# Opening loop of a hybrid conv/retention block: VectorE in place of GpSimd, ScalarE for scale and shift, part of the modulation as one-column matmuls

## The chip, the cores and the metric

The kernel runs on one core of one Trainium2 chip. The metric is device time in microseconds (us): the time of one execution as the runs report it. For the kernel before, three runs were timed. The profile comes from one further execution on the chip. Its engines are TensorE (PE, with weight loads listed apart as PEld), VectorE (DVE), ScalarE (ACT), GpSimd (POOL) and SyncE (SP), which issues the DMA transfers here.

## The reference

One layer of an encoder, batch 1, 2048 tokens, width 1024, float32 throughout. What matters here is its first part:

```python
mod = silu(c) @ w_ada + b_ada                 # 1024 -> 6 * 1024
shift1, scale1, gate1, shift2, scale2, gate2 = split(mod, 6)
h = rms_norm(x, g_pre_mix) * (1.0 + scale1) + shift1
xin, b_gate, c_gate, q, k, v, g = split(h @ w_in)     # seven groups of 512 columns
```

Behind it come a short causal convolution, a chunked retention with rotary q and k, an output projection, and an MLP with a squared ReLU, each with its modulation, norm and residual. The modulation is a vector of 1024 numbers per part: the whole row of `silu(c)` times a column of `w_ada`, so a sum over 1024 products for each.

## The kernel before, in words

Tokens are worked in four blocks of 512. The width of 1024 is split into eight k tiles of 128 partitions. A GEMM of a 128x128 weight tile with a 128x512 moving tile is done as three matmuls in a rounded float32 form, on the high and low halves of both operands: line 142 is high by high, line 143 high by low, line 144 low by high. In the opening the activations h are the stationary operand, so that line 143 uses the low half of the weights (`wlo`) and line 144 the low half of h. The trace names the other operand as well: `g<-wlo,r` is line 143.

The opening is the block of code under the pool `st`, for the first 512 tokens. It runs as follows.

- The eight tiles of x, transposed, are loaded (line 277). ScalarE squares each (line 280), VectorE adds the squares up in `sacc` (line 282), and four one-column matmuls with a column of ones (line 285) give the sum of squares of each token.
- `rstd` makes the inverse root: VectorE scales (line 125), GpSimd takes the power of -0.5 (line 127). `spread` lays it out along the tokens: VectorE multiplies the identity by it, four 128x128 pieces (line 223), one matmul with ones (line 227) spreads it over all partitions, ScalarE copies it to `rb` (line 229).
- `mod1(kt)` makes the scale and shift sums of k tile kt. It loads two tiles of 128 x 4 x 256 numbers of `w_ada` (tag `ada`, eight buffers, line 193) and VectorE multiplies each of the eight 128x256 pieces by one column of `silu(c)` and adds them up in `pt` (lines 197 and 199). The sum over the partitions is left to TensorE.
- `mod1_end(kt, pt)` sums `pt` over the partitions by two one-column matmuls (line 207; the profile shows them as four records, since each float32 matmul has two), one for the scale and one for the shift, into two columns of `modps`. All eight k tiles share this one PSUM bank, and the matmuls of a tile wait until the columns before have been read. VectorE then makes `a1 = (sum + 1 + b) * g_pre_mix` (line 210) and `sh1 = sum + b` (line 214).
- `h0_tile(k, pts)` calls `mod1_end`, multiplies the tile of x by `rb` (line 296: VectorE for tile 0, GpSimd for the other seven), and lets ScalarE make h = x * a1 + sh1 twice, as the rounded high half and in full (line 299). VectorE subtracts them to the low half (line 303).
- `startup_weights(kp)` loads the V and K weights of two k tiles (two tiles of 128x1024, line 134). ScalarE rounds them to the high half (line 136), and GpSimd subtracts to the low half (line 138). K weights come from `st` with two buffers, V weights from `wp` with three.
- The loop over the eight k tiles then does seven GEMM groups for each, into seven PSUM banks that stay open over all eight: V for four token tiles and K for three, 7 x 3 matmuls a tile. The call of `h0_tile(k + 1)` stands behind the second group, that of `mod1(k + 2)` ahead of the first.

Each engine works through its own instructions in an order that is fixed before the run. The framework's scheduler chooses it, by an estimate of when each instruction can start and by the order of the program among those that can; a line further down the program may go first. In the trace, for instance, VectorE does four products of tile 0 (from 13.38 us) ahead of line 125. SyncE also issues in order: a load that waits for its buffer holds those behind it.

Behind the opening come the copies of V (line 555), the rotary tables on VectorE (from line 362, in memory that the opening's pools give back), the rotary itself (lines 530 and 539) and the remaining GEMMs of the first block. Some loads are tied to the last load of `mod1` (`last`) by `issue_after`.

Of the kernel before, what the change touches and what calls it, by code (L numbers as in the profile page):

```python
# [11 lines left out]
F32 = mybir.dt.float32  # L12
F32R = mybir.dt.float32r
I32 = mybir.dt.int32
AF = mybir.ActivationFunctionType
ALU = mybir.AluOpType

P = 128
# [3 lines left out]
NK = D // P  # L22
# [12 lines left out]
XIN, BG, CG, QQ, KK, VV, GG = range(7)  # L35
# [19 lines left out]
def block_kernel(  # L55
# [5 lines left out]
    nc = tc.nc  # L61
    PS = bass.MemoryType.PSUM

    keep = ctx.enter_context(tc.tile_pool(name="keep", bufs=1))
# [12 lines left out]
    def nm(s):  # L77
        n_of[s] = n_of.get(s, 0) + 1
        return f"{s}_{n_of[s]}"

    def tmp(shape=(P, 512), dt=F32):
        name = nm("tmp")
        return tp.tile(list(shape), dt, tag="tmp" + "ab"[n_of["tmp"] % 2], name=name, bufs=4)
# [10 lines left out]
    def bank(shape=(P, 512)):  # L94
        return gp.tile(list(shape), F32, tag="g", name=nm("g"))

    def mbank(shape=(P, 512)):
        return mp.tile(list(shape), F32, tag="m", name=nm("m"))
# [4 lines left out]
    ones = keep.tile([P, P], F32, name="ones")  # L103
# [11 lines left out]
    bcol_sb = keep.tile([P, 4, NK], F32, name="bcol_sb")  # L115
    nc.sync.dma_start(bcol_sb, bcol)
    gcol_sb = keep.tile([P, 2, NK], F32, name="gcol_sb")
    nc.sync.dma_start(gcol_sb, gcol)
    sc = keep.tile([P, NK], F32, name="sc")
    nc.scalar.activation(sc, c_sb, AF.Silu)  # L120

    def rstd(ss, n, inv, tag):

        ms = small([P, n], tag + "m")
        nc.vector.tensor_scalar(ms, ss, inv, EPS, op0=ALU.mult, op1=ALU.add)
        r = small([P, n], tag + "r")
        nc.gpsimd.tensor_tensor(r, ms, negh[:, 0:n], op=ALU.pow)
        return r


    def wgroup(src, eng=None, pool=None):
        pool, n = (wp, 3) if pool is None else (pool, 2)
        raw = pool.tile([P, 1024], F32, tag="raw", name=nm("raw"), bufs=n)
        nc.sync.dma_start(raw, src)
        hi = pool.tile([P, 1024], F32R, tag="whi", name=nm("whi"), bufs=n)
        nc.scalar.copy(hi, raw)  # L136
        lo = pool.tile([P, 1024], F32R, tag="wlo", name=nm("wlo"), bufs=n)
        (eng or nc.vector).tensor_tensor(lo, raw, hi.bitcast(F32), op=ALU.subtract)  # L138
        return hi, lo

    def mm3(ps, ah, al, bh, bl, first, last):
        nc.tensor.matmul(ps, ah, bh, start=first, stop=False)  # L142
        nc.tensor.matmul(ps, ah, bl, start=False, stop=False)  # L143
        nc.tensor.matmul(ps, al, bh, start=False, stop=last)  # L144
# [34 lines left out]
    bs1 = keep.tile([P, NK], F32, name="bs1")  # L179
# [3 lines left out]
    a1 = keep.tile([P, NK], F32, name="a1")  # L183
    sh1 = keep.tile([P, NK], F32, name="sh1")
    a2 = keep.tile([P, NK], F32, name="a2")
    sh2 = keep.tile([P, NK], F32, name="sh2")

    def mod1(kt):

        pt = st.tile([P, 256], F32, tag="pt", name=nm("pt"), bufs=4)  # L190
        for i in range(2):
            raw = st.tile([P, 4, 256], F32, tag="ada", name=nm("ada"), bufs=8)
            last = nc.sync.dma_start(raw, ada1[kt, i].rearrange("p (k c) -> p k c", k=4))
            for k in range(4):
                c_ = sc[:, 4 * i + k : 4 * i + k + 1]
                if i == k == 0:
                    nc.vector.tensor_scalar(pt, raw[:, k, :], c_, None, op0=ALU.mult)
                else:
                    nc.vector.scalar_tensor_tensor(  # L199
                        pt, raw[:, k, :], c_, pt, op0=ALU.mult, op1=ALU.add  # L200
                    )
        return pt, last

    def mod1_end(kt, pt):
        ps = modps[:, 2 * kt : 2 * kt + 2]
        for w in range(2):
            nc.tensor.matmul(
                ps[:, w : w + 1], pt[:, w * P : w * P + P], ones[:, 0:1], start=True, stop=True
            )
        nc.vector.scalar_tensor_tensor(  # L210
            a1[:, kt : kt + 1], ps[:, 0:1], bs1[:, kt : kt + 1], gcol_sb[:, 0, kt : kt + 1],
            op0=ALU.add, op1=ALU.mult,
        )
        nc.vector.tensor_tensor(
            sh1[:, kt : kt + 1], ps[:, 1:2], bcol_sb[:, 0, kt : kt + 1], op=ALU.add
        )


    def spread(r):

        dg = tmp()
        for t in range(NT):
            nc.vector.tensor_scalar(
                dg[:, t * P : t * P + P], ident, r[:, t : t + 1], None, op0=ALU.mult
            )
        ps = mbank()
        nc.tensor.matmul(ps, ones, dg, start=True, stop=True)
        rb = tmp()
        nc.scalar.copy(rb, ps)
        return rb  # L230
# [20 lines left out]
    def h_(tag, dt=F32R):  # L251
        return hp.tile([P, 512], dt, tag=tag, name=nm(tag), bufs=HP[tag])
# [19 lines left out]
    with tc.tile_pool(name="st", bufs=NK) as st:  # L272
        xts = []
        sacc = st.tile([P, TB], F32, tag="sacc", name="sacc", bufs=1)
        for k in range(NK):
            xt = st.tile([P, TB], F32, tag="x0", name=nm("x0"))
            nc.sync.dma_start(xt, xT[k * P : k * P + P, 0:TB])
            xts.append(xt)
            sq = sacc if k == 0 else tmp()
            nc.scalar.activation(sq, xt, AF.Square)  # L280
            if k > 0:
                nc.vector.tensor_tensor(sacc, sacc, sq, op=ALU.add)
        ps = mbank()
        for t in range(NT):
            nc.tensor.matmul(
                ps[:, t : t + 1], sacc[:, t * P : t * P + P], ones[:, 0:1], start=True, stop=True
            )
        rb = spread(rstd(ps[:, 0:NT], NT, 1.0 / D, "r1"))
        modps = mbank()
        extra = mbank()  # L290

        def h0_tile(k, pts):
            mod1_end(k, pts)
            h = tmp()
            eng = nc.vector if k == 0 else nc.gpsimd
            eng.tensor_tensor(xts[k], xts[k], rb, op=ALU.mult)
            hi = h_("r" if k < 5 else "wh")
            for o in (hi, h):
                nc.scalar.activation(
                    o, xts[k], AF.Identity, scale=a1[:, k : k + 1], bias=sh1[:, k : k + 1]  # L300
                )
            lo = h_("r" if k < 5 else "wl")
            nc.vector.tensor_tensor(lo, h, hi.bitcast(F32), op=ALU.subtract)
            h_cur.append((hi, lo))


        def startup_weights(kp):
            return [wgroup(win[c * 4 + kp], nc.gpsimd, pool) for c, pool in ((VV, None), (KK, st))]

        pts, _ = mod1(0)  # L310
        ws = startup_weights(0)
        nxt, last = mod1(1)
        h0_tile(0, pts)
        start_ps = [bank() for _ in range(6)] + [extra]
        for k in range(NK):
            if k % 2 == 0 and k > 0:
                ws = startup_weights(k // 2)
            pts = nxt
            if k + 2 < NK:
                nxt, last = mod1(k + 2)  # L320
            c = slice(k % 2 * 512, k % 2 * 512 + 512)
            xh, xl = h_cur[k]
            for i, (w, t) in enumerate([(0, t) for t in range(NT)] + [(1, t) for t in range(3)]):
                if i == 2 and k + 1 < NK:
                    h0_tile(k + 1, pts)
                s = slice(t * P, t * P + P)
                hi, lo = ws[w]
                mm3(start_ps[i], xh[:, s], xl[:, s], hi[:, c], lo[:, c], k == 0, k == NK - 1)
# [5 lines left out]
    def at(tag, shape=(P, 512), dt=F32, bufs=4):  # L334
        pool = {"yh": pl, "yl": pl, "kT": late, "sg": late}.get(tag, pa)
        return pool.tile(list(shape), dt, tag=tag, name=nm(tag), bufs=bufs)
# [178 lines left out]
    with pa_stack:  # L515
# [30 lines left out]
        for b in range(NB):  # L546
# [72 lines left out]
            for t in range(NT):  # L619
                ps = mbank()  # L620
                for h in range(H):
                    s = slice(h * P, h * P + P)
# [4 lines left out]
                if b * NT + t < SEQ // P - 1:  # L627
                    ps = mbank()
                    for h in range(H):
                        s = slice(h * P, h * P + P)  # L630
# [4 lines left out]
                    else:  # L635
                        for h in range(H):
                            s = slice(h * P, h * P + P)
# [4 lines left out]
                for h in range(H):  # L642
                    s = slice(h * P, h * P + P)
# [21 lines left out]
            for j, ps in enumerate(gemm_t(w_in(CG), h_cur)):  # L665
# [4 lines left out]
                c_ = at("qT")  # L670
# [9 lines left out]
            for t in range(NT):  # L680
# [5 lines left out]
                for h in range(H):  # L686
                    s = slice(h * P, h * P + P)
                    o = slice(t * P, t * P + P)
# [23 lines left out]
            for ch, tag in enumerate(("kT", "sg")):  # L712
# [7 lines left out]
                if ch == 0:  # L720
# [3 lines left out]
                    if b + 1 < NB:  # L724
                        rb = spread(r1)
# [448 lines left out]
```

## Time and profile before

| | before |
|---|---|
| median of three runs | 2238.92 us (2238.62 to 2243.34) |
| profiled execution, its own time | 2240.46 us |
| profiled execution, span first to last instruction | 2238.7 us |
| TensorE matmul busy | 2143.6 us (96%) |
| VectorE busy | 1442.8 us (64%) |
| ScalarE busy | 989.9 us (44%) |
| GpSimd busy | 586.7 us (26%) |
| TensorE's mean granted clock | 0.988 |

In the rows of the profile, L138 is line 138 of the kernel; `out<-in` are the program's names without buffer numbers; x8 is a count of instructions; in the timeline the first two numbers are start and length in us, and a bracket tells how long the engine had been idle and what ended that. A start of a matmul is exact, its end is modelled, so that matmuls in a stream seem to overlap: their pace is read from start to start. In the waits, a row is "engine tile line <- engine tile line" with the total, the number of waits and the longest. Times inside the kernel are counted from the first instruction.

### The profile page before, as it was taken

The page shows a single profiled execution, that of the slowest core. Times are in us where ns is not written, and L with a number is a line of the kernel's source. Part 1 is how long each engine was busy: PE and PEld are TensorE (multiplying, and loading weights), DVE is VectorE, ACT ScalarE, POOL GpSimd, SP SyncE. Part 2 cuts the span into 40 slices and gives each one's busy share as a digit, 9 for nine tenths or more (in the row PEclk, how much of TensorE's full clock was granted, in tenths as well). Part 3 has the DMA queues.
Part 4 walks back from the last instruction along what each step waited for, and adds up shares of the span by engine and source line. Part 5 has one row for each costly group of instructions (what it writes and reads, how often), then busy time and mean ns, then how long its engine had stood idle before and what let it go on. Part 6 is the DMA issues. An engine that isn't in the chain of part 4 may idle for free.

```text
span 2238.7 us, 28424 instructions
## 1 busy us (share of the span) xinstructions
PE 2143.6 (96%) x9736; PEld 1765.9 (79%) x9736; DVE 1442.8 (64%) x2198; ACT 989.9 (44%) x1714; POOL 586.7 (26%) x441
## 2 busy tenths in 40 slices
PE   3999999999999999989999999999999999999997
PEld 2787877878787888867888878888888888888885
DVE  7766845675567634776666687556776666555566
ACT  3332532244224522466555556444445555454453
POOL 4132254314423351243333300001433333010012
PEclk8999999999999999999999999999999999999999
DMA  7356467546655563566444477666764443666666
GB/s 283 132 179 220 157 229 242 177 143 214 212 174 202 182 229 129 200 209 217 150 151 148 135 231 219 204 194 192 259 229 155 150 154 120 211 190 197 196 191 242
DMA packets 197426, 428.23 MB, mean 191 GB/s; under 512 B 22560, under 2 KB 22560, under 8 KB 197280
## 3 DMA queue, kind: packets, MB, share of 16 engines
q1 hardware_dynamic: 197280, 426.41, 57.7%
q8 instruction: 76, 1.25, 0.2%
q14 instruction: 70, 0.57, 0.1%
HBM read 322.51 MB, written 103.81 MB: 190 GB/s over the span
## 4 chain that ended last, share of the span: by engine, by line
PE 67%; DMA 11%; issue 10%; DVE 7%; POOL 3%; ACT 1%; SPq 0%; DVEq 0%; POOLq 0%; ACTq 0%
PE g L142 20%; PE g L143 20%; PE g L144 20%; DMA w2r<-in_w 2%; DMA w2d<-w2r 2%; DMA fw<-fd 2%; PE m L142 2%; PE m L143 2%; PE m L144 2%; POOL w2r L502 2%; DMA ada<-in_ada 1%; DMA x<-in_x 1%; DVE pt L199 1%; DVE wl L807 1%; DVE ql L807 1%
## 5 line engine op out<-in xcount | busy, mean ns | idle before, releaser
L143 PE MATMUL g<-ql,wh 128*128 128x512 f32 x896 | 350.9, 392 | 9.6 <-DVE ql L807 9.6
L144 PE MATMUL g<-qh,wl 128*128 128x512 f32 x896 | 350.9, 392 | 0.5 <-DVE wl L807 0.4
L142 PE MATMUL g<-qh,wh 128*128 128x512 f32 x896 | 350.2, 391 | 0.1
L136 ACT CAST whi<-raw 128x1024 fp32r<-128x1024 f32 x148 | 155.3, 1052 | 348.5 <-PE g L144 178.4
L872 DVE TENSOR_TENSOR q<-g,q 128x512 f32<-128x512 f32 x267 | 178.4, 687 | 174.8 <-PE g L144 174.6
L138 DVE TENSOR_TENSOR wlo<-raw,whi 128x1024 fp32r<-128x1024 f32 x140 | 187.6, 1344 | 152.2 <-ACT whi L136 151.7
L807 DVE TENSOR_TENSOR fl<-fw,fh 128x512 fp32r<-128x512 f32 x218 | 161.3, 741 | 162.5 <-ACT fh L806 160.3
L143 PE MATMUL g<-wl,fh 128*128 128x512 f32 x680 | 265.3, 390 | 0.3 <-DVE wl L807 0.3
L144 PE MATMUL g<-wh,fl 128*128 128x512 f32 x680 | 264.6, 389 | 0.0
L806 ACT CAST fh<-fw 128x512 fp32r<-128x512 f32 x218 | 135.2, 620 | 225.8 <-DMA fw<-fd 213.1
L806 ACT CAST wh<-r 128x512 fp32r<-128x512 f32 x224 | 138.8, 620 | 214.7 <-PE g L143 188.7
L142 PE MATMUL g<-wh,fh 128*128 128x512 f32 x680 | 218.4, 390 | 0.8 <-ACT wh L806 0.8
L143 PEld LDWEIGHTS g<-ql,wh 128*128 128x128 f32 x896 | 169.0, 189 | 46.6 <-DVE ql L807 11.5
L144 PEld LDWEIGHTS g<-qh,wl 128*128 128x128 f32 x896 | 169.1, 189 | 36.3 <-DVE wl L807 1.9
L142 PEld LDWEIGHTS g<-qh,wh 128*128 128x128 f32 x896 | 169.3, 189 | 36.1 <-ACT qh L806 0.7
L807 DVE TENSOR_TENSOR wl<-fw,wh 128x512 fp32r<-128x512 f32 x218 | 156.2, 717 | 44.7 <-ACT wh L806 42.2
L1005 POOL TENSOR_TENSOR q<-q,gg 128x512 f32<-128x512 f32 x28 | 43.4, 1577 | 533.4 <-ACT q L1002 285.3
L807 DVE TENSOR_TENSOR wl<-r,wh 128x512 fp32r<-128x512 f32 x224 | 163.6, 731 | 11.0 <-ACT wh L806 10.8
L806 ACT CAST wh<-fw 128x512 fp32r<-128x512 f32 x218 | 135.0, 619 | 65.3 <-PE g L144 30.3
L890 POOL TENSOR_TENSOR r<-r,r 128x512 f32<-128x512 f32 x32 | 41.4, 1294 | 431.8 <-DVE wl L807 384.3
L143 PEld LDWEIGHTS g<-wl,fh 128*128 128x128 f32 x680 | 127.6, 188 | 29.4 <-DVE wl L807 2.9
L142 PEld LDWEIGHTS g<-wh,fh 128*128 128x128 f32 x680 | 127.4, 188 | 28.2 <-ACT wh L806 2.0
(257 smaller groups left out, 4448.6 us busy)
## 6 DMA issues: line engine op xcount, KB each, us to landing
raw<-in_win SPq DMA_DIRECT2D x116, 512.0 KB, 4.2
fd<-q SPq DMA_DIRECT2D x224, 256.0 KB, 2.2
fw<-fd SPq DMA_DIRECT2D x224, 256.0 KB, 2.8
r<-in_w SPq DMA_DIRECT2D x128, 256.0 KB, 4.7
fw<-w2d SPq DMA_DIRECT2D x128, 256.0 KB, 3.0
ada<-in_ada SPq DMA_DIRECT2D x48, 512.0 KB, 4.7
fw<-in_w SPq DMA_DIRECT2D x96, 256.0 KB, 3.6
w2r<-in_w SPq DMA_DIRECT2D x32, 512.0 KB, 5.4
```

Of the source, the lines that this page charges most:

```text
L136: nc.scalar.copy(hi, raw)
L138: (eng or nc.vector).tensor_tensor(lo, raw, hi.bitcast(F32), op=ALU.subtract)
L142: nc.tensor.matmul(ps, ah, bh, start=first, stop=False)
L143: nc.tensor.matmul(ps, ah, bl, start=False, stop=False)
L144: nc.tensor.matmul(ps, al, bh, start=False, stop=last)
L199: nc.vector.scalar_tensor_tensor(pt, raw[:, k, :], c_, pt, op0=ALU.mult, op1=ALU.add)
L502: nc.gpsimd.tensor_tensor(o, a, b_, op=ALU.subtract)
L806: nc.scalar.copy(hi, src)
L807: nc.vector.tensor_tensor(lo, src, hi.bitcast(F32), op=SUB)
L872: (eng or nc.vector).tensor_tensor(o, a, b_, op=ADD)
L890: nc.gpsimd.tensor_tensor(b11, b12, b11, op=SUB)
L1005: eng.tensor_tensor(c, c, gg[1][:, j * 512 : j * 512 + 512], op=ALU.mult)
```

## The change

- `mod1(kt)` now sums only the first n of the eight products on VectorE, n = 4, 4, 6, 7, 7, 8, 8, 8 for k tiles 0 to 7. The rest stay as raw pieces of the loaded tiles.
- `mod1_end` takes those raw pieces to TensorE: for each, and for scale and shift, a one-column matmul of the 128x128 piece with its column of `silu(c)`, accumulated with the sum of `pt` in the same PSUM column. That is twelve products, 24 matmuls.
- `a1` and `sh1` are made on ScalarE, from PSUM: `a1` as sum * g + (1 + b) * g, for which VectorE makes `bs1g = bs1 * g` once at the start, and `sh1` as sum + b.
- The scaling of x by `rb` is done on VectorE for all eight tiles. It is called in `scaled(k)`, ahead of `mod1(k)`, no more in `h0_tile`.
- The weight differences of `startup_weights` are made on VectorE.

```diff
--- before.py
+++ after.py
@@ -185,35 +185,42 @@
     a2 = keep.tile([P, NK], F32, name="a2")
     sh2 = keep.tile([P, NK], F32, name="sh2")
 
+    bs1g = keep.tile([P, NK], F32, name="bs1g")
+    nc.vector.tensor_tensor(bs1g, bs1, gcol_sb[:, 0, :], op=ALU.mult)
+
     def mod1(kt):
 
+
+        n = NK - (4, 4, 2, 1, 1, 0, 0, 0)[kt]
         pt = st.tile([P, 256], F32, tag="pt", name=nm("pt"), bufs=4)
+        raws = []
         for i in range(2):
             raw = st.tile([P, 4, 256], F32, tag="ada", name=nm("ada"), bufs=8)
             last = nc.sync.dma_start(raw, ada1[kt, i].rearrange("p (k c) -> p k c", k=4))
-            for k in range(4):
-                c_ = sc[:, 4 * i + k : 4 * i + k + 1]
-                if i == k == 0:
-                    nc.vector.tensor_scalar(pt, raw[:, k, :], c_, None, op0=ALU.mult)
-                else:
-                    nc.vector.scalar_tensor_tensor(
-                        pt, raw[:, k, :], c_, pt, op0=ALU.mult, op1=ALU.add
-                    )
-        return pt, last
-
-    def mod1_end(kt, pt):
+            raws += [raw[:, k, :] for k in range(4)]
+        for k, raw in enumerate(raws[:n]):
+            c_ = sc[:, k : k + 1]
+            if k == 0:
+                nc.vector.tensor_scalar(pt, raw, c_, None, op0=ALU.mult)
+            else:
+                nc.vector.scalar_tensor_tensor(pt, raw, c_, pt, op0=ALU.mult, op1=ALU.add)
+        return (pt, list(enumerate(raws))[n:]), last
+
+    def mod1_end(kt, parts):
+        pt, raws = parts
         ps = modps[:, 2 * kt : 2 * kt + 2]
         for w in range(2):
-            nc.tensor.matmul(
-                ps[:, w : w + 1], pt[:, w * P : w * P + P], ones[:, 0:1], start=True, stop=True
-            )
-        nc.vector.scalar_tensor_tensor(
-            a1[:, kt : kt + 1], ps[:, 0:1], bs1[:, kt : kt + 1], gcol_sb[:, 0, kt : kt + 1],
-            op0=ALU.add, op1=ALU.mult,
+            s = slice(w * P, w * P + P)
+            for k, raw in raws:
+                nc.tensor.matmul(
+                    ps[:, w : w + 1], raw[:, s], sc[:, k : k + 1], start=k == raws[0][0], stop=False
+                )
+            nc.tensor.matmul(ps[:, w : w + 1], pt[:, s], ones[:, 0:1], start=not raws, stop=True)
+        o = slice(kt, kt + 1)
+        nc.scalar.activation(
+            a1[:, o], ps[:, 0:1], AF.Identity, scale=gcol_sb[:, 0, o], bias=bs1g[:, o]
         )
-        nc.vector.tensor_tensor(
-            sh1[:, kt : kt + 1], ps[:, 1:2], bcol_sb[:, 0, kt : kt + 1], op=ALU.add
-        )
+        nc.scalar.activation(sh1[:, o], ps[:, 1:2], AF.Identity, bias=bcol_sb[:, 0, o])
 
 
     def spread(r):
@@ -292,8 +299,6 @@
         def h0_tile(k, pts):
             mod1_end(k, pts)
             h = tmp()
-            eng = nc.vector if k == 0 else nc.gpsimd
-            eng.tensor_tensor(xts[k], xts[k], rb, op=ALU.mult)
             hi = h_("r" if k < 5 else "wh")
             for o in (hi, h):
                 nc.scalar.activation(
@@ -305,10 +310,15 @@
 
 
         def startup_weights(kp):
-            return [wgroup(win[c * 4 + kp], nc.gpsimd, pool) for c, pool in ((VV, None), (KK, st))]
-
+            return [wgroup(win[c * 4 + kp], None, pool) for c, pool in ((VV, None), (KK, st))]
+
+        def scaled(k):
+            nc.vector.tensor_tensor(xts[k], xts[k], rb, op=ALU.mult)
+
+        scaled(0)
         pts, _ = mod1(0)
         ws = startup_weights(0)
+        scaled(1)
         nxt, last = mod1(1)
         h0_tile(0, pts)
         start_ps = [bank() for _ in range(6)] + [extra]
@@ -317,6 +327,7 @@
                 ws = startup_weights(k // 2)
             pts = nxt
             if k + 2 < NK:
+                scaled(k + 2)
                 nxt, last = mod1(k + 2)
             c = slice(k % 2 * 512, k % 2 * 512 + 512)
             xh, xl = h_cur[k]
```

## Prediction

> **What bounds the kernel now.** I began with the page, for the span and the forms of the work, and went from it to the opening, which alone the change touches. The GEMMs run on TensorE, so an edit elsewhere wins back only time in which TensorE stands still. How much of that the opening holds is told by the waits of TensorE in the first 89 us (us in total, times, longest).
>
> ```profile
> span 2238.7 us, 28424 instructions
> PE m L285 <- DVE sacc L282: 13.5, 1, 13.5
> PE m L227 <- DVE tmp L223: 6.7, 1, 6.7
> PE g L144 <- DVE r L303: 6.1, 1, 6.1
> PE m L207 <- DVE sh L214: 4.5, 2, 4.1
> PE g L142 <- ACT r L299: 4.2, 1, 4.2
> ```
>
> The first wait is for x and its squares, which the change leaves alone. The other four, 21.5 us, end on work that VectorE does or releases. Next I cut the opening at its events, the first GEMM matmul, the first matmul of the second k tile and the last matmul, into windows (columns: PE, PEld, DVE, ACT, POOL busy, then clock, DMA share, GB/s).
>
> ```profile
> 28.87:50.50 21.63, 11.07 (x33) 8.84 (x33) 19.84 (x26) 5.61 (x7) 13.54 (x8) 0.67 0.50 187
> 50.50:88.92 38.42, 38.42 (x165) 31.43 (x164) 25.45 (x51) 14.02 (x18) 7.25 (x3) 0.92 0.44 161
> ```
>
> From 50.50 on TensorE has no gap until the opening ends at 88.92. Between 28.87 and 50.50 it is half idle while VectorE is busy 19.84 of 21.63 us. The timeline of VectorE and that of GpSimd beside it say with what:
>
> ```profile
> 12.64 0.69 DVE L282 TENSOR_TENSOR sacc<-sacc,tmp 128x512 f32<-128x512 f32 x1 [0.28 <-ACT tmp L280]
> 16.87 5.06 DVE L223 TENSOR_SCALAR tmp<-ident,r1r 128x128 f32<-128x128 f32 x4
> 30.60 6.84 DVE L199 SCALAR_TENSOR_TENSOR pt<-ada,sc,pt 128x256 f32<-128x256 f32 x4
> 37.37 2.82 DVE L303 TENSOR_TENSOR r<-tmp,r 128x512 fp32r<-128x512 f32 x1
> 43.28 4.81 DVE L199 SCALAR_TENSOR_TENSOR pt<-ada,sc,pt 128x256 f32<-128x256 f32 x11
> 48.00 0.21 DVE L210 SCALAR_TENSOR_TENSOR a<-m,bs,gcol_sb 128x1 f32<-128x1 f32 x1
> ...
> 15.67 1.14 POOL L127 TENSOR_TENSOR r1r<-r1m,negh 128x4 f32<-128x4 f32 x1 [14.10 <-DVE r1m L125]
> 17.00 4.65 POOL L138 TENSOR_TENSOR wlo<-raw,whi 128x1024 fp32r<-128x1024 f32 x2 [0.19 <-ACT whi L136]
> 24.76 9.93 POOL L296 TENSOR_TENSOR x<-x,tmp 128x512 f32<-128x512 f32 x7 [3.11 <-ACT tmp L229]
> 34.65 7.76 POOL L138 TENSOR_TENSOR wlo<-raw,whi 128x1024 fp32r<-128x1024 f32 x3
> ```
>
> Wherever GpSimd runs, VectorE is slow: four products take 6.84 us beside it and eleven take 4.81 us once it is done. The minima of the same lines, by source, are the prices without GpSimd (ns, min/median/max):
>
> ```profile
> L197 DVE TENSOR_SCALAR pt<-ada,sc x8: 342/344/2491, 13.4 to 66.3; 128x256 f32<-128x256 f32 x8
> L199 DVE SCALAR_TENSOR_TENSOR pt<-ada,sc,pt x56: 471/484/2607, 13.8 to 71.3; 128x256 f32<-128x256 f32 x56
> L223 DVE TENSOR_SCALAR tmp<-ident,r1r x4: 274/1326/2376, 16.9 to 21.7; 128x128 f32<-128x128 f32 x4
> L303 DVE TENSOR_TENSOR r<-tmp,r x5: 680/684/2822, 37.4 to 68.5; 128x512 fp32r<-128x512 f32 x5
> L138 DVE TENSOR_TENSOR wlo<-raw,whi x5: 1215/1225/1226, 72.5 to 94.0; 128x1024 fp32r<-128x1024 f32 x5
> ```
>
> So the opening is bound by VectorE held up by GpSimd until 50.50, then by TensorE.
>
> **The change, part by part.** *VectorE.* It takes over eight weight differences (8 x 1.225 = 9.8 us) and seven scalings of x, each priced as the 128x512 sum of row 12.64 (8 x 0.69 = 5.5 us with the one it has). It loses 12 of 64 products (12 x 0.484 = 5.8 us) and the sixteen short a1/sh1 instructions. From 13.38 on, behind row 12.64, it has 8 x 0.344 + 44 x 0.484 = 24.0 us of products, 9.8, 5.5, 8 x 0.684 = 5.5 for line 303 and 4 x 0.274 = 1.1 for line 223: 45.9 us, which would end at 59.3 if it never waited. With GpSimd gone from the stage no row leaves a reason for the long forms.
>
> *The path to the first GEMM matmul.* These rows carry it:
>
> ```profile
> 15.35 0.16 DVE L125 TENSOR_SCALAR r1m<-m 128x4 f32<-128x4 f32 x1
> 21.98 2.08 PE L227 MATMUL m<-tmp,ones 128*128 128x512 f32 x2 [6.67 <-DVE tmp L223]
> 24.10 0.59 ACT L229 COPY tmp<-m 128x512 f32<-128x512 f32 x1 [5.93 <-PE m L227]
> 28.01 0.81 ACT L299 ACTIVATE r<-x,sh,a 128x512 fp32r<-128x512 f32 x1 [3.32 <-DVE x L296]
> 28.87 0.80 PE L142 MATMUL g<-whi,r 128*128 128x512 f32 x1 [4.17 <-ACT r L299]
> 48.33 1.02 PE L207 MATMUL m<-ones,pt 128*128 128x1 f32 x4 [4.08 <-DVE sh L214]
> ```
>
> The power on GpSimd still ends at 16.81; the four diagonals then end at 16.87 + 1.1 = 18.0 instead of 21.93, the spreading matmul at 20.1, its copy at 20.7, the scaling of tile 0 at 21.4, the ScalarE activation at 22.3: the floor is 22.35. But tile 0 now needs five pairs of one-column matmuls (four raw, one pt), 1.02 us a pair at the slow clock of row 48.33, 5.1 us in all. TensorE has 2.5 us for them between 15.5 and 18.0; the other 2.6 us stand before or behind the spreading matmul. Before it, the first matmul comes at 24.9; behind it at 18.0 + 2.1 + 2.6 + 0.5 for two ScalarE instructions + 0.9 = 24.1. I take 24.5. If none fits in the gap it is 27.4. The gain is 28.87 - 24.5 = 4.4 us, between 1.5 and 6.5.
>
> The two ScalarE instructions per tile are not in the trace; bounds are the 128x8 and the 128x512 activation:
>
> ```profile
> L120 ACT ACTIVATE sc<-c_sb 128x8 f32<-128x8 f32 x1 | 0.2, 208 | 0.6 <-DMA c_sb<-in_cT 0.6
> ```
>
> so 0.21 to 0.81 us each, and I take 0.25, by the small form. Queued behind them on ScalarE are that tile's two activations and the weight casts; ScalarE is busy 14 of 38 us in the window from 50.50, which covers it. What they free is larger: a1 of tile 1 was not written before 48.00, behind eleven products in VectorE's queue, and TensorE's next pair waited for that (the 4.1 us of L207). On ScalarE no product stands ahead of it.
>
> *From the first matmul to the end of the opening.* These rows give the pace, slow and full, and a pair of one-column matmuls in the stream:
>
> ```profile
> 30.75 0.63 PE L142 MATMUL g<-whi,r 128*128 128x512 f32 x1
> 32.45 0.54 PE L142 MATMUL g<-whi,r 128*128 128x512 f32 x1
> 64.46 0.50 PE L207 MATMUL m<-ones,pt 128*128 128x1 f32 x4
> 64.82 0.49 PE L142 MATMUL g<-whi,r 128*128 128x512 f32 x1
> 65.14 0.40 PE L143 MATMUL g<-wlo,r 128*128 128x512 f32 x1
> 101.13 0.39 PE L143 MATMUL g<-wlo,r 128*128 128x512 f32 x1
> 107.48 0.39 PE L144 MATMUL g<-whi,wl 128*128 128x512 f32 x1
> ```
>
> Between the last two lie 28 steps: 0.227 us each. The opening has 8 tiles x 7 groups x 3 = 168 such matmuls, 38.1 us. A pair costs 0.36 us (64.46 to 64.82), up to 0.45 with the matmul behind it; tiles 1 to 7 have 8 raw and 7 pt pairs, 15 x 0.40 = 6.0 us, of which 8 pairs, 3.2 us, are new. The slow pace is four steps from 30.75 to 32.45, 0.43 us each, 0.2 more than full. It lasted from 28.87 to 32.45, where the matmuls begin to shorten: 3.6 us, 1.7 of them lost. In the window from 50.50 the mean clock of 0.92 over 38.42 us means 3.1 us lost, 6.2 us at half. I put in one stretch, the mean of the two losses, 2.4 us. VectorE's 46 us run ahead of TensorE's pace, so I leave only 2.0 us for waits, a fifth of the present 6.1 + 4.5. The opening ends at 24.5 + 38.1 + 6.0 + 2.4 + 2.0 = 73.0 instead of 88.92: 15.9 us earlier.
>
> [...]
>
> *Queues and DMA.* The modulation tiles share eight buffers; those whose products go to TensorE are now freed by TensorE, and SyncE, which issues in order, holds the next weight load behind such a wait.
>
> ```profile
> 42.72 5.71 SPq L193 DMA_DIRECT2D ada<-in_ada  x5
> ```
>
> Today five of these loads leave at 42.72 or later. After the change tile 1's products are out of TensorE near 30, so its buffers pass on earlier than now: nothing on this account, and a few us if tile 1 is late.
>
> *Behind the opening.* VectorE's rotary tables start when the opening's last matmul ends and TensorE waits for them:
>
> ```profile
> 89.18 0.42 DVE L362 TENSOR_TENSOR wide<-cst_sb,pos_f 128x256 f32<-128x256 f32 x1 [7.18 <-PE m L144]
> 110.53 0.47 PE L142 MATMUL g<-whi,r 128*128 128x512 f32 x1 [2.66 <-DVE tmp L539]
> ```
>
> That chain hangs on the end of the opening, so it moves as a whole. VectorE is idle for 7.18 us ahead of it; that cover shrinks but stays, since its work ends before TensorE's. What changes here is only the order in which the scheduler mixes later work: 0, with 3 us either way.
>
> **The rivals.** *Stop and go.* VectorE's queue order again holds TensorE between tiles: half the present 10.6 us recur (5.3 in place of 2.0), with both slow stretches (1.7 + 3.1 in place of 2.4) and the late start of 27.4 (2.9 us more): 8.6 us of the gain lost. For it: 46 us of VectorE work is close to the 48.5 us that TensorE's opening takes. Against it: the long rows all stand beside GpSimd. Gain 7.3 us.
>
> *Given back.* The opening ends early, but the later order costs as much: for it, the gap of 2.66 us at 110 shows that the next stage hangs on VectorE; against, that stage starts from the opening's last matmul, so only the order within it can give time back, and it would have to give back six times that gap. No change.
>
> *Slower: the one-column matmuls keep TensorE at half clock.* They stand in TensorE's queue in front of GEMM matmuls and wait for loads, for VectorE's pt and for ScalarE's reading of the one PSUM bank that all tiles share; the clock falls in each gap, as after the 6.1 us wait. The point at which this eats the gain is 15.9 / 0.2 = 80 of the 168 matmuls at 0.43 us. With all of them, a first matmul at 27.4, 168 x 0.43 and 15 x 1.02 us, the opening ends at 114.9: 26 us slower. For it: the pair at 48.33 took 1.02 us against 0.36 later, and the 6.2 us behind 50.50 were slow without any gap. [...]
>
> *No release.* If VectorE's long rows were not GpSimd's doing, VectorE's net new work (9.8 + 4.8 - 5.8 = 8.8 us) would come on top of what holds TensorE now and the time would be 2248; the 274 against 2376 ns of one instruction speaks so strongly against it that its chance is counted in the slower case.
>
> **How the numbers follow.** The profiled execution took 2240.46 us (span 2238.7 and 1.8 around it), 0.07% above the median of 2238.92; 2240.46 - 15.9 = 2224.6, on the median's scale 2238.92 - 15.9 = 2223.0. The forecast has 0.67; its own range has the floor of 22.35 with pairs of 0.36 us, no slow stretch and no wait (end 65.9, gain 23.1: 2216) and a late start of 27.4, pairs of 0.45, 3.1 lost to the slow clock and 5 to waits (end 80.4, gain 8.5: 2230). Stop and go has 0.17 at 2231.6, given back 0.09 at 2239, slower 0.07 at 2265. The range 2214 to 2234 takes in the first two with 2 to 3 us of later order on either side. This kernel's measurement can tell 0.2%, 4.5 us, from no change: faster 0.85, same 0.08, slower 0.07.
>
> **What would show it.** Right: no GpSimd row of lines 138 or 296 before the opening ends; line 223 at four times 0.28 us; the first GEMM matmul near 24.5; the waits of L144 for L303 and of L207 nearly gone; last opening matmul near 73; a rotary wait still near 2.7 us. Wrong: line 303 or the products still above 1 us; one-column matmuls with waits of several us; matmul starts 0.43 us apart beyond 40 us; an opening that ends early with a span that does not follow.

## The result, and the profile after

Six runs of the changed kernel have a median of 2221.07 us (2219.15 to 2222.68), six of the kernel before 2238.77 us: a ratio of 0.9923, 95% interval 0.9909 to 0.9936, so 17 us faster. Beside the later experiments the same kernel ran twice more, at 0.9939 (0.9924 to 0.9953) and 0.9937 (0.9924 to 0.9951), 14 us faster. The forecast was 2223.0, 15.9 us. Two executions that lie far outside all the others, one of the kernel before at 3640.62 us and one of the changed kernel at 5592.29 us, are left out of the ratios.

The page gives the new span; TensorE's waits in the first 75 us stand below it, in the form shown of before.

```profile
span 2217.9 us, 28512 instructions
```

```profile
PE m L292 <- DVE sacc L289: 13.8, 1, 13.8
PE m L234 <- DVE tmp L230: 2.4, 1, 2.4
PE m L215 <- ACT sh L223: 1.2, 2, 0.6
```

The first wait is the old one, for x. Of the other four, 21.5 us, there remain 3.6 us. The lines have new numbers: 230 are the diagonals (223 before), 215 the raw one-column matmuls, 218 the pair with pt, 220 and 223 scale and shift on ScalarE, 308 the low half of h, 316 the scaling. The windows are cut at the same events as before, the last two cuts up to 0.3 us behind them: first GEMM matmul, first of the second k tile, end of the opening, end of the rotary wait; columns as before.

```profile
0.00:26.42 26.42, 9.70 (x39) 8.53 (x39) 16.27 (x33) 11.46 (x18) 2.04 (x12) 1.00 0.88 328
26.42:37.41 10.99, 10.40 (x47) 8.71 (x47) 10.80 (x22) 4.69 (x7) 0.00 (x0) 1.00 1.03 409
37.41:74.40 36.99, 36.99 (x177) 30.63 (x176) 21.80 (x41) 18.20 (x31) 0.00 (x0) 1.00 0.48 186
74.40:95.00 20.60, 18.30 (x81) 14.87 (x81) 18.47 (x39) 7.51 (x11) 1.19 (x2) 1.00 0.47 153
95.00:2217.90 2122.90, 2067.98 (x9448) 1707.23 (x9446) 1368.06 (x2054) 953.60 (x1665) 555.94 (x413) 0.99 0.58 191
```

The stretch of the first k tile, 21.63 us before, takes 10.99 us, and TensorE is busy for 10.40 of them. The clock column reads 1.00 there and also from 28.87 to 32.45 before, although the matmul starts lie 0.43 us apart until 32.11 and until 32.45; for the slow pace of the start only the pace can be read. The start comes 2.45 us earlier (28.87 to 26.42), the other seven k tiles take 1.6 us less. The last matmul of the opening starts at 74.02, so with the pace of 0.23 it ends near 74.25 against 88.92: 14.7 us of the 20.8 by which the two profiled spans differ. Another 1.2 us lie in the stretch to the end of the rotary wait (21.61 us before, 94.69 - 74.25 = 20.44 after); the rotary wait at its end fell from 2.66 to 1.58 us. Behind it the kernel before takes this long:

```profile
110.53:2238.70 2128.17, 2071.43 (x9448) 1707.70 (x9448) 1360.24 (x2054) 952.43 (x1665) 554.57 (x413) 0.99 0.58 190
```

and the changed one 2217.9 - 94.69 = 2123.2 us. Of these last 5.0 us little can be put down to the change: in its second and third profile the same kernel takes 2125.8 and 2127.3 us from that point on.

GpSimd's timeline from 12 to 90 us has two rows left, and VectorE's shows the short forms beside them:

```profile
15.96 1.04 POOL L127 TENSOR_TENSOR r1r<-r1m,negh 128x4 f32<-128x4 f32 x1 [14.39 <-DVE r1m L125]
74.63 0.82 POOL L679 COPY u<-halo 128x2 f32<-128x2 f32 x1 [57.63 <-PE m L144]
```

```profile
17.04 0.87 DVE L230 TENSOR_SCALAR tmp<-ident,r1r 128x128 f32<-128x128 f32 x4 [1.23 <-POOL r1r L127]
20.69 1.29 DVE L316 TENSOR_TENSOR x<-x,tmp 128x512 f32<-128x512 f32 x2 [0.25 <-ACT tmp L236]
22.30 3.70 DVE L316 TENSOR_TENSOR x<-x,tmp 128x512 f32<-128x512 f32 x6
26.83 0.69 DVE L308 TENSOR_TENSOR r<-tmp,r 128x512 fp32r<-128x512 f32 x1
27.44 2.46 DVE L206 SCALAR_TENSOR_TENSOR pt<-ada,sc,pt 128x256 f32<-128x256 f32 x6
```

The diagonals take 0.87 us for four (5.06 before), the low half of tile 0 takes 0.69 (2.82), six products 2.46 (four took 6.84). The scheduler put all eight scalings together, from 20.69 to 26.0, with a single product between them. TensorE's timeline shows where the start lost what it did not win, with ScalarE's two new instructions beside it:

```profile
17.96 2.08 PE L234 MATMUL m<-tmp,ones 128*128 128x512 f32 x2 [2.36 <-DVE tmp L230]
19.83 1.71 PE L215 MATMUL m<-sc,ada 128*128 128x1 f32 x8
21.40 0.57 PE L218 MATMUL m<-ones,pt 128*128 128x1 f32 x2
21.83 1.84 PE L215 MATMUL m<-sc,ada 128*128 128x1 f32 x8
23.53 0.56 PE L218 MATMUL m<-ones,pt 128*128 128x1 f32 x2
24.69 1.86 PE L215 MATMUL m<-sc,ada 128*128 128x1 f32 x8 [0.59 <-ACT sh L223]
26.42 0.77 PE L142 MATMUL g<-whi,r 128*128 128x512 f32 x1
32.11 0.49 PE L143 MATMUL m<-wlo,r 128*128 128x512 f32 x1
```

```profile
24.14 0.35 ACT L220 ACTIVATE a<-m,bs1g,gcol_sb 128x1 f32<-128x1 f32 x1 [3.47 <-PE m L218]
24.39 0.25 ACT L223 ACTIVATE sh<-m,bcol_sb 128x1 f32<-128x1 f32 x1
```

The spreading matmul starts at 17.96, as worked out (18.0). All five pairs of tile 0 stand behind it, 19.83 to 24.09, none in the gap ahead of it, and four raw matmuls of tile 1 (24.69, x8 records) stand ahead of the first GEMM matmul too, although tile 0's activation (24.67 and 0.81 us) was done at 25.5.

### The profile page after: what moved, and what is told of

The parts are those of the page before. It is cut to its first block, busy times and chain, and to the rows that moved or that the text cites. A ratio compares the mean times of both kernels' runs of the same rounds, so it can differ in the third digit from the quotient of the medians.

```text
span 2217.9 us, 28512 instructions
## 1 busy us (share of the span) xinstructions
PE 2143.4 (97%) x9784; PEld 1770.0 (80%) x9784; DVE 1435.4 (65%) x2186; ACT 995.5 (45%) x1730; POOL 559.2 (25%) x426
## 4 chain that ended last, share of the span: by engine, by line
PE 70%; issue 11%; DMA 9%; DVE 4%; POOL 4%; ACT 1%; SPq 1%; DVEq 0%; POOLq 0%; ACTq 0%
PE g L142 20%; PE g L144 20%; PE g L143 20%; DMA w2r<-in_w 2%; PE m L142 2%; PE m L143 2%; PE m L144 2%; POOL w2r L513 2%; DMA w2d<-w2r 2%; DMA x<-in_x 1%; DMA ada<-in_ada 1%; DMA q<-h2d 1%; DVE wl L818 1%; DVE ql L818 1%; POOL sg L753 1%
## 5 line engine op out<-in xcount | busy, mean ns | idle before, releaser
L138 DVE TENSOR_TENSOR wlo<-raw,whi 128x1024 fp32r<-128x1024 f32 x148 | 200.5, 1360 | 159.0 <-ACT whi L136 157.9
```

## The experiments

The theory at the start (A): the gain is GpSimd's release, scale and shift on ScalarE add to it, and the raw one-column matmuls cost about what they bring. The rivals were that the twelve products taken from VectorE win the time (B), and that what GpSimd made was waited for, not that it ran. The table gives for each kernel the start of the first GEMM matmul, that of the first GEMM matmul behind the opening (in the profile), and the time as a ratio to the kernel before with its interval.

| kernel | first GEMM matmul | next stage | ratio |
|---|---|---|---|
| before | 28.87 | 89.88 | 1 |
| changed | 26.42 | 75.12 | 0.9923 (0.9909 to 0.9936) |
| a_again | 26.46 | 76.00 | 0.9939 (0.9924 to 0.9953) |
| a_third | 25.91 | 75.47 | 0.9937 (0.9924 to 0.9951) |
| e1, all products on VectorE | 22.34 | 78.50 | 0.9949 (0.9931 to 0.9966) |
| e2, scale and shift on VectorE | 28.57 | 76.54 | 0.9944 (0.9931 to 0.9957) |
| e3, weight differences on GpSimd | 33.27 | 84.19 | 0.9981 (0.9972 to 0.9990) |
| e4, scaling on GpSimd | 29.17 | 78.05 | 0.9933 (0.9919 to 0.9948) |
| e5, only GpSimd's work moved | 23.70 | 79.65 | 0.9959 (0.9943 to 0.9975) |
| e6, idle work on GpSimd added | 27.65 | 82.43 | 0.9977 (0.9966 to 0.9988) |
| e7a, tile 0 on VectorE | 22.52 | 71.84 | 0.9926 (0.9914 to 0.9938) |
| e8a, and later scalings held back | 22.36 | 71.66 | 0.9927 (0.9911 to 0.9944) |
| e8a_again | 23.15 | 72.57 | 0.9930 (0.9913 to 0.9947) |

**e1: all products on VectorE.**

```diff
-        n = NK - (4, 4, 2, 1, 1, 0, 0, 0)[kt]
+        n = NK - (0, 0, 0, 0, 0, 0, 0, 0)[kt]
```

> The changed kernel with all 64 products on VectorE, no one-column matmuls of raw pieces; GpSimd still out, scale and shift still on ScalarE. Theory A (the gain is GpSimd's release; the raw one-column matmuls cost as much as they bring): they stand between the spreading matmul (ended 20.0) and the first GEMM matmul (26.42) in the changed kernel, 4.3 us of tile 0 and 1.9 us of tile 1; without them the first GEMM matmul comes near 23 and the whole is within 3 us of the changed kernel, rather faster (2218 to 2222). Theory B (taking 12 products, 5.8 us, from VectorE is what wins the time): TensorE waits for VectorE's products again, the opening ends 4 to 6 us later, 2225 to 2228.

The first GEMM matmul came early, even more than A had it, but TensorE then stood still. From its timeline:

```profile
22.34 0.80 PE L142 MATMUL g<-whi,r 128*128 128x512 f32 x1 [1.72 <-ACT r L304]
28.89 0.39 PE L144 MATMUL m<-whi,r 128*128 128x512 f32 x1
36.77 1.01 PE L218 MATMUL m<-ones,pt 128*128 128x1 f32 x4 [7.49 <-DVE pt L206]
```

After tile 0 (28.89) it waits 7.49 us for tile 1's products, which VectorE does behind eight scalings, weight differences and the products of tiles 2 and 3 that the scheduler mixed in. The next stage starts some 3 us later than in the changed kernel's three profiles (75.1 to 76.0), less than B's 4 to 6. A's number fails here and B's sign holds: in the opening the raw matmuls as a whole do pay, through the wait for tile 1. Over the whole kernel the intervals overlap.

**e2: scale and shift on VectorE.**

```diff
-        nc.scalar.activation(a1[:, o], ps[:, 0:1], AF.Identity, scale=..., bias=bs1g[:, o])
-        nc.scalar.activation(sh1[:, o], ps[:, 1:2], AF.Identity, bias=bcol_sb[:, 0, o])
+        nc.vector.scalar_tensor_tensor(a1[:, o], ps[:, 0:1], bs1[:, o], gcol_sb[:, 0, o], ...)
+        nc.vector.tensor_tensor(sh1[:, o], ps[:, 1:2], bcol_sb[:, 0, o], op=ALU.add)
```

> The changed kernel with a1 and sh1 back on VectorE. Theory A (their move out of VectorE's queue counts beside GpSimd's release): a1 of a tile stands behind products again, TensorE's one-column matmuls wait for sh several us in total, the opening ends 2 to 5 us later, 2223 to 2226. Rival: with GpSimd gone VectorE's queue is never far behind, and the wait stays under 1 us: 2221 within 2.

```profile
26.84 1.87 PE L215 MATMUL m<-sc,ada 128*128 128x1 f32 x8 [2.81 <-DVE sh L223]
```

TensorE waits 2.81 us for a shift that stands behind six scalings in VectorE's queue; the first GEMM matmul comes 2.2 us later (28.57). At the next stage about 1 us of that is left (0.5 to 1.4, by the three profiles). The queue effect is there, the rival's wait of under 1 us is not, and A's loss of 2 to 5 us in the opening did not come either; over the whole kernel the intervals overlap.

**e3 and e4: one part back on GpSimd.**

```diff
+ e3: wgroup(win[c * 4 + kp], nc.gpsimd, pool)
+ e4: (nc.vector if k == 0 else nc.gpsimd).tensor_tensor(xts[k], xts[k], rb, op=ALU.mult)
```

> The changed kernel with the eight weight differences back on GpSimd, 2.4 us each, the scaling still on VectorE. Theory A (a VectorE instruction with two SBUF operands stands still while GpSimd runs one): VectorE loses about as long as GpSimd works in the first 60 us, some 15 to 20 us, and is relieved of 9.8 us; the spreading diagonals take some 4 to 5 us again (0.87 in the changed kernel) and the opening ends 5 to 9 us later: 2226 to 2230. Rival (GpSimd's scaling alone was the harm): no change or a little faster, 2217 to 2222.

> The changed kernel with the scaling of tiles 1 to 7 back on GpSimd (10 us of GpSimd work from about 21 us on), the weight differences still on VectorE. Theory A: products beside it take 1.4 us instead of 0.48, VectorE falls 6 to 7 us behind less the 4.8 us it is relieved of; the opening ends 1 to 5 us later: 2222 to 2226. Rival (the weight differences alone were the harm): 2221 within 1.

VectorE's timeline in e3, with GpSimd's first row, and then VectorE's in e4:

```profile
17.15 5.05 DVE L230 TENSOR_SCALAR tmp<-ident,r1r 128x128 f32<-128x128 f32 x4 [1.23 <-POOL r1r L127]
31.33 10.95 DVE L206 SCALAR_TENSOR_TENSOR pt<-ada,sc,pt 128x256 f32<-128x256 f32 x11
...
17.08 4.64 POOL L138 TENSOR_TENSOR wlo<-raw,whi 128x1024 fp32r<-128x1024 f32 x2
```

```profile
25.04 6.77 DVE L206 SCALAR_TENSOR_TENSOR pt<-ada,sc,pt 128x256 f32<-128x256 f32 x6
```

In e3 the diagonals take 5.05 us again, eleven products 10.95 us, and the next stage starts some 9 us later; most of the gain is gone. The opening lost what A expected, the whole more (2235.5). In e4 six products take 6.77 us against 2.46, and the next stage starts 2.5 us later; over the whole kernel the loss does not stand out of the interval.

**e5: only GpSimd's work moved.** e1 and e2 together: the kernel before with lines 138 and 296 on VectorE, the scaling called ahead of `mod1` as in the changed kernel.

> The kernel before with GpSimd's work moved to VectorE and nothing else: all 64 products, a1 and sh1 stay on VectorE. Taken one by one from the changed kernel, the products cost 5.8 us and the scale and shift 4.7 us. Theory A (GpSimd's release is the larger half): still 5 to 9 us faster than the kernel before. Rival (the parts only work together: VectorE's 46 us plus 5.8 and 2.9 us are then what the opening lasts): within 3 us of the kernel before.

The next stage starts 10.2 us earlier than before (79.65 against 89.88) and the whole is 0.41% faster, 9.2 us: a little above A's range, and some seven tenths of the 13.9 to 14.8 us that the whole change wins in the opening. What is left to win is this wait:

```profile
PE m L218 <- DVE pt L206: 8.3, 2, 6.5
```

**e6: GpSimd work that nobody waits for.**

```diff
+    nc.gpsimd.tensor_tensor(idle, hi[:, s], hi[:, s], op=ALU.subtract)   # two per weight tile, 16 in all
```

The rest of the kernel is the changed one; the extra results are not used.

> The changed kernel with sixteen subtractions more on GpSimd in the opening, 128x512 with two SBUF operands, whose result nobody reads (about 21 us of GpSimd work). Theory A (GpSimd's work in itself stops VectorE's two-operand instructions): the four diagonals take 4 to 5 us again, products beside it 1 us and more, the opening ends 4 to 9 us later. Rival (what cost the time before was waiting for what GpSimd made, not its running): no change, within 1 us.

VectorE's timeline and then GpSimd's:

```profile
16.70 2.44 DVE L230 TENSOR_SCALAR tmp<-ident,r1r 128x128 f32<-128x128 f32 x4 [1.23 <-POOL r1r L127]
31.53 5.59 DVE L206 SCALAR_TENSOR_TENSOR pt<-ada,sc,pt 128x256 f32<-128x256 f32 x6
```

```profile
28.50 7.55 POOL L320 TENSOR_TENSOR idle<-whi 128x512 f32<-128x512 f32 x6 [5.35 <-ACT whi L136]
```

Six products take 5.59 us beside it against 2.46 in the changed kernel, the diagonals 2.44 against 0.87 (less than the 4 to 5 of A), and the next stage starts 6.4 us after that of a_again on the same chip. The whole is some 8.5 us slower, and the two intervals lie apart. The new subtractions read the weights, so they could also have held a weight buffer back, but up to 85 us no engine and no load waited for them. What TensorE waited for is VectorE's products:

```profile
PE m L218 <- DVE pt L206: 3.4, 1, 3.4
```

So GpSimd's running alone, with results that nobody reads, is what held VectorE up here: products went from 0.41 us each (2.46 for six) to 0.93 (5.59 for six). This decides against the rival.

**e7a and e8a: a start without tile 0's raw matmuls.** e7a changes the first count, e8a also holds back the scaling of tiles 2 to 7 until the products of the tile before are issued.

```diff
-        n = NK - (4, 4, 2, 1, 1, 0, 0, 0)[kt]
+        n = NK - (0, 4, 2, 1, 1, 0, 0, 0)[kt]
+                with tc.issue_after(done[k + 1].ins):     # e8a only: last product of tile k + 1
                     scaled(k + 2)
```

> The changed kernel with tile 0 summed on VectorE alone (0 4 2 1 1 of 8 on TensorE) and the scaling of tiles 2 to 7 held behind the products of the tile before. With all products on VectorE the first GEMM matmul came at 22.34, but TensorE then waited 7.5 us for tile 1, whose products stood behind the scaling of all eight tiles (20.7 to 26). Theory: the first GEMM matmul comes near 23.3 instead of 26.42, tile 1 near 34 instead of 37.4, and the whole is 2 to 4 us faster than the changed kernel. Rival: VectorE is full until 57 us whatever the order, and TensorE waits for a later tile instead: no gain.

> The changed kernel with tile 0 summed on VectorE alone (0 4 2 1 1 of 8 on TensorE); the scaling is left where the scheduler puts it. Theory (the raw one-column matmuls of tile 0 only delay the first GEMM matmul, those of tile 1 save a wait): the first GEMM matmul comes at 22.4 and tile 1 some 2 us earlier than in the changed kernel, with a short wait for tile 1's products, which stand behind the scalings; the opening ends 1 to 3 us earlier. Rival: without the scaling held back TensorE waits for tile 1 as long as it gained, no change.

> The version with tile 0 on VectorE and late scaling once more beside the changed kernel: its opening ended 4.3 us earlier than the changed kernel's, the whole came out 2.6 us lower with overlapping intervals. If the rest behind the opening is the same but for chance, 3 to 5 us below the changed kernel; if the later order is dearer in this version, 0 to 2 us.

The reference for these, and for e5 and e6, was the changed kernel itself:

> The changed kernel once more, to stand beside the next three on one chip: 0.992 of the kernel before, as measured.

> The changed kernel a third time, for the next two: 0.992 to 0.994 of the kernel before.

e7a's start and its next stage, from TensorE's timeline, then e8a's:

```profile
22.52 0.77 PE L142 MATMUL g<-whi,r 128*128 128x512 f32 x1
71.84 0.50 PE L142 MATMUL g<-whi,r 128*128 128x512 f32 x1 [0.72 <-ACT va L566]
```

```profile
22.36 0.77 PE L142 MATMUL g<-whi,r 128*128 128x512 f32 x1
71.66 0.50 PE L142 MATMUL g<-whi,r 128*128 128x512 f32 x1 [0.72 <-ACT va L571]
```

Both win 3 to 4 us more in the opening, above the 1 to 3 forecast for e7a, so tile 0's raw matmuls are a loss. Those of tiles 1 to 4 are not: e1, which lacks them as well, starts the next stage 6.7 us after e7a. No run takes out those of tile 1 alone. Holding the scalings back adds nothing to that: e8a's start and end are e7a's. As whole kernels they come out at 0.9926, 0.9927 and 0.9930, some 1.5 to 3 us below the changed kernel run beside them, with intervals that overlap. From the end of the rotary wait on they take 2128 to 2130 us, the changed kernel 2123 to 2127. Whether that is their later order or chance is open.

## Why the prediction was right, step by step

The bound was read rightly: VectorE, held up by GpSimd, until the second k tile, then TensorE. The long forms went with GpSimd, and e6 shows that they come back with it.

The start was the weakest step. Its terms were close (spreading matmul 17.96 for 18.0; five pairs 4.3 us for 5.1; scale and shift 0.35 and 0.25 us for 0.25 each), but the assumption that 2.5 us of one-column matmuls fit in the gap ahead of the spreading matmul was wrong: the scheduler's order put none there, and tile 1's first set besides ahead of the GEMM. The first GEMM matmul came at 26.42 in place of 24.5, inside the 27.4 given for that case.

Behind the start the sum was 48.5 us and the trace has 74.25 - 26.42 = 47.8. Of its terms the 2.0 us for waits were too many (0.6 us were left), the slow pace cost 13 matmuls x 0.2 = 2.6 us for 2.4, and some 6.5 us remain for the pairs of one-column matmuls for 6.0, although two of the fifteen pairs already stood ahead of the start. So the opening ended at 74.25 for 73.0, a gain of 14.7 for 15.9, and the whole at 0.9923 to 0.9939 for 0.9929. That the whole came so near is in part luck: a start 1.9 us late was largely offset by 1.4 us of waits that did not come, and time won behind the opening, which the sum had at nothing, covered what was missing. That e1 lost shows a point the prediction did not weigh: VectorE's total of 46 us was right to be called uncritical, but its order was not. The products taken from tiles 1 to 4 are together worth more than their 0.48 us each. In e1 tile 1 is the only one whose products TensorE came to wait for, so the worth is probably in getting that tile out early, which is argued and not tested. Those of tile 0 are worth less than nothing.

Of the rivals, stop and go is what e1 and e5 look like, given back did not happen, and a little of the slower one shows, as a second stretch at half clock in the later profiles (last section). That the rest of the kernel took 1.2 us less up to the rotary and 1 to 5 us less behind it was inside the 3 us allowed for order, or nearly; 2.6 and 4.1 of the 5.0 us did not come again.

## What to carry to other kernels

Price an elementwise instruction on GpSimd by what it takes from VectorE while it runs, not by its own time: here 9.8 and 4.8 us of added VectorE work bought a 10 us earlier end. When work is spread over engines, ask for each tile whether the engine that takes it is the one the first result waits for: raw products on TensorE helped at tiles 1 to 4, taken together, and hurt at tile 0. A busy total that fits says nothing on order; look for the one instruction that stands behind a batch moved forward by the scheduler.

## What the runs showed of the hardware

In the kernel before, from 17 to 42 us, twelve VectorE instructions of 128x128 to 128x512 (lines 197, 199, 223, 296 and 303) began while GpSimd ran a weight difference or a scaling, and each took 1.38 to 2.82 us, about the length of the GpSimd instruction (1.26 to 2.80), whatever its own: beside differences of 2.3 to 2.8 us the diagonal of 274 ns took up to 2376 and the low half of h 2822 instead of 680. The diagonals have a single tile as input, so that the two operands in the theory of e3 and e6 are no condition that these rows show. Nor was VectorE slow beside everything that GpSimd ran: the 128x1 shift of line 214 kept its 0.15 us at 26.23, beside a scaling, and three products took 1.52 us at 15.43, beside the 128x4 power of line 127 (15.67, 1.14 us), as three did ahead of it (13.77, 1.53 us). Beside e6's subtractions, 1.14 us in the median, single products took 1.26 us (28.70, 53.63 and 56.80) instead of 0.48. Once in e6 it went the other way: at 30.93 us both engines begin one, the low half of h keeps its 0.68 us, and the GpSimd subtraction takes 1.57 us:

```profile
30.93 0.68 DVE L308 TENSOR_TENSOR r<-tmp,r 128x512 fp32r<-128x512 f32 x1
30.93 1.57 POOL L320 TENSOR_TENSOR idle<-whi 128x512 f32<-128x512 f32 x1
```

After a stretch of one-column matmuls the fast pace was lost. In a_again TensorE ran at full pace up to 33.3, did one-column matmuls of tiles 1 and 2 until 36.6 with one wait of 0.59 us, and fell back to steps of 0.43 us within a microsecond of the next GEMM matmul:

```profile
34.34 0.36 PE L218 MATMUL m<-ones,pt 128*128 128x1 f32 x2
35.30 0.61 PE L215 MATMUL m<-sc,ada 128*128 128x1 f32 x4 [0.59 <-ACT sh L223]
36.66 0.49 PE L142 MATMUL g<-whi,r 128*128 128x512 f32 x1
37.86 0.63 PE L142 MATMUL g<-whi,r 128*128 128x512 f32 x1
38.28 0.63 PE L143 MATMUL g<-wlo,r 128*128 128x512 f32 x1
40.84 0.41 PE L143 MATMUL g<-wlo,r 128*128 128x512 f32 x1
```

It lasted until 40.84, some 8 steps or 1.6 us lost. The granted clock of that window, the third number from the end, says the same:

```profile
37.45:40.84 3.39, 3.39 (x9) 2.65 (x8) 3.32 (x8) 1.44 (x2) 0.00 (x0) 0.50 1.04 412
```

The profiles of a_third, e7a, e8a and e8a_again have such a stretch behind tile 1's one-column matmuls too, steps of 0.43 us for 3.0 us from 37.22, 32.51, 33.27 and 34.08; the first profile of the changed kernel does not, and why is open. In the kernel before the half clock came within the wait of 6.1 us that ended at 40.25:

```profile
32.00:36.00 4.00, 2.15 (x8) 1.41 (x6) 4.00 (x4) 0.35 (x1) 4.00 (x3) 1.00 0.27 110
36.00:40.00 4.00, 0.00 (x0) 0.00 (x0) 4.00 (x2) 0.00 (x0) 4.00 (x3) 0.52 0.00 0
```

In a_again TensorE was idle for no more than 0.6 us at a time ahead of its slow stretch, by the waits. Whether the one-column matmuls brought it about is not shown: no run tests that by itself. The start says less: the first 13 GEMM matmuls of the changed kernel, from 26.42 to 32.11, ran at the slow pace behind 6 us of one-column matmuls, but the first ones of e1, with no raw matmuls ahead of them, did so too, from 22.34 to 26.35.
